# Splitting the rotary high-high terms of attention scores into pairs of half-array matmuls

## The chip, the core and the metric

The kernel runs on one core of a Trainium2 chip. The metric is the time of one execution on the device in microseconds (us). Engines are named as in the profile: PE is TensorE (matmuls), PEld its weight loads, DVE is VectorE, ACT is ScalarE, POOL is GpSimd, SP issues transfers.

## What is computed

One layer of an encoder: an RMS norm, one input projection, three token mixers (a convolution, a retention with two scan directions, latent attention), a gate, an output projection with the residual, a last RMS norm; 1024 tokens, 1024 channels, float32. The change touches the scores of the latent attention alone (8 heads, 1024 queries by 1024 keys):

```
def attend(blk):
    qn, qr = blk
    s = (jnp.einsum('bqhd,bkhd->bhqk', qn, k_nope)     # 128 channels per head
         + jnp.einsum('bqhr,bkr->bhqk', qr, k_rope))   # 64 rotary channels, key shared by all heads
    p = jax.nn.softmax(s.astype(jnp.float32) * scale, axis=-1).astype(v.dtype)
    return jnp.einsum('bhqk,bkhd->bqhd', p, v)
```

## The kernel before

Every float32 matmul operand is held as two fp32r tiles, high and low: the high tile is a cast, the low tile the rest (`split_l` on DVE). A product is then the sum of high-high, high-low and low-high passes into one PSUM bank (`mm3`, lines 174 to 176). A *pass* below is one matmul of a 128x128 stationary tile over 512 moving columns, together with its own weight load.

The program first computes the input projection with the convolution and the retention, then the attention, then the output projection. The attention is a loop over 16 units (`Unit`, line 795): unit u has head u // 2 and query half u % 2, which is four blocks of 128 queries. For each block t, `qk` makes the scores S, a PSUM tile of two banks, one bank for each half of 512 keys (j = 0, 1). A bank takes five passes: three for the 128 plain channels (L811 to L813: high-high, high-low, low-high) and two for the 64 rotary channels (L814, L815). The rotary operands use 128 array rows for 64 channels: the tile `Q2` (named QA or QB in the trace, by head) holds the low part of the query in rows 0 to 63 and its high part in rows 64 to 127. `K2` holds the key's high part in rows 0 to 63 and its low part in rows 64 to 127, and `K3` the other way round. So the pass with K2 gives low-high plus high-low, the pass with K3 low-low plus high-high. In the trace K2 and K3 are both called K.

After the second bank DVE takes the row maximum (L818), ACT the exponential with the row sums (L820), PE transposes the probabilities (`tr`, L829, two lots of four 128x128 transposes), ACT and DVE split them into PH and PL. The product with the values (`pvs`, mm3) and the normalization (`norm`, with one transpose of a 128x4 tile, L841) of a unit run in the next unit. `g_kr` (line 718) makes K2 and K3 once; `g_r` and `g_r2` make the rotated query tiles of a head pair; `slot_plan` spreads these and the projections of the next heads over the units.

The order that a reader of the code sees is not the order that runs: a scheduler puts the instructions of each engine into a row of its own. S has two buffers (of two banks), the transposes have two. The program gives every matmul a tile of the array: 128x128 for all but the 20 transposes of narrow tiles (16 of L841), which have 128x32.

Of the kernel before, what the change touches and what calls it, by code (L numbers as in the profile page):

```python
# [8 lines left out]
F32 = mybir.dt.float32  # L9
# [10 lines left out]
HS = 512  # L20
# [35 lines left out]
def body(tc, xT, x, w_in, w_uqn, w_uqr, w_uk, w_uv, w_out, vecs, decay, final_g,  # L56
         t_ret, t_mla, t_idx, t_iota, idm, out):
    nc = tc.nc
    act, dve, pool, pe, sp = nc.scalar, nc.vector, nc.gpsimd, nc.tensor, nc.sync

    def stt(eng, o, a, s, b, op0, op1):
        eng.scalar_tensor_tensor(o, a, s, b, op0=op0, op1=op1)  # L62
# [4 lines left out]
    def split_l(eng, lo, src, hi, scale=1.0):  # L67
        stt(eng, lo, src, scale, hi.bitcast(F32), MUL, SUB)
# [8 lines left out]
    def ps(tag, w=HS):  # L77
        cnt[0] += 1
        return psp[0].tile([P, w], F32, name=f"ps{cnt[0]}", tag=tag, bufs=PSB[tag])
# [13 lines left out]
    def mk(pl, shape, dt=F32, tag=None, bufs=None):  # L93
        cnt[0] += 1
        kw = {} if bufs is None else {"bufs": bufs}
        return pl.tile(shape, dt, name=f"{tag}{cnt[0]}", tag=tag, **kw)
# [569 lines left out]
    def half(i):  # L666
        return slice(i * HS, (i + 1) * HS)
# [42 lines left out]
    K2 = mk(at, [P, S], F32R, tag="K2")  # L710
    K3 = mk(at, [P, S], F32R, tag="K3")
    kk, qq, q2, vv = {}, {}, {}, {}
# [5 lines left out]
    def g_kr():  # L718
        for h in range(2):
            o = ps_up()  # L720
            pe.matmul(o, i2, krt[h], start=True, stop=True)
            act.copy(K2[0:64, half(h)], o[0:64])
            act.copy(K3[64:128, half(h)], o[64:128])
            split_l(dve, K2[64:128, half(h)], o[64:128], K3[64:128, half(h)])
            split_l(dve, K3[0:64, half(h)], o[0:64], K2[0:64, half(h)])

    def ps_up():
        tag = PRO_.pop(0) if PRO_ else "up"
        return ps(tag, 2 * HS)[:, :HS] if tag == "S" else ps(tag)
# [65 lines left out]
    class Unit:  # L795
# [6 lines left out]
        def qk(self, i):  # L802
            t, j = i // 2, i % 2
            if j == 0:
                self.S = ps("S", 2 * HS)
            kh, kl = kk[self.h, j]
            qh, ql = qq[self.h, self.qh]
            Q2 = q2[self.h, self.qh]
            ts = slice(t * P, (t + 1) * P)
            o = self.S[:, half(j)]  # L810
            pe.matmul(o, qh[:, ts], kh, start=True, stop=False)  # L811
            pe.matmul(o, qh[:, ts], kl, start=False, stop=False)  # L812
            pe.matmul(o, ql[:, ts], kh, start=False, stop=False)  # L813
            pe.matmul(o, Q2[:, ts], K2[:, half(j)], start=False, stop=False)  # L814
            pe.matmul(o, Q2[:, ts], K3[:, half(j)], start=False, stop=True)  # L815
            if j == 1:
                nm = mk(at, [P, 1], tag="nm", bufs=4)
                dve.tensor_reduce(nm, self.S, axis=AX.X, op=MAX, negate=True)  # L818
                p = mk(at, [P, S], tag="P", bufs=P_BUFS)
                act.activation(p, self.S, AF.Exp, bias=nm, accum_out=self.rs[:, t:t + 1])  # L820
                self.p.append(p)

        def tr(self, t, j):
            if t == 0:
                self.PT[j] = [mk(at, [P, 4, HS], F32R, tag=g, bufs=PT_BUFS) for g in ("PH", "PL")]
            ph, pl = (v[:, :, t * P:(t + 1) * P] for v in self.PT[j])
            o = ps("pp")
            for c in range(4):
                pe.transpose(o[:, c * P:(c + 1) * P], self.p[t][:, (4 * j + c) * P:(4 * j + c + 1) * P], ident)  # L829
            o = o.rearrange("p (c q) -> p c q", c=4)  # L830
            act.copy(ph, o)  # L831
            split_l(dve, pl, o, ph)
# [37 lines left out]
    for i in range(QT):  # L870
        lat(i, 1)
    g_q(0, 0)
    g_kr()
    g_r2(0, 0)
    g_r(0, 1)
# [4 lines left out]
    def slot_plan(u):  # L880
        p, r = u // 4, u % 4
        a, b = 2 * p, 2 * p + 1
        last = p == MH // 2 - 1
        if r == 0:
            return {0: [lambda: W.update({("k", b): lw_k(b)}), lambda: g_q(a, 1)],
                    4: [lambda: g_v(p, 1)], 5: [lambda: g_v(p, 2)],
                    6: [lambda: W.update({("q", b): lw_q(b)})],
                    7: [lambda: g_v(p, 3)]}
        if r == 1:
            d = {0: [lambda: g_k(b, 0)], 1: [lambda: g_k(b, 1)], 4: [lambda: g_q(b, 0)]}  # L890
            if not last:
                d[2] = [lambda: W.update({("r", p + 1): lw_r(p + 1)})]
                d[6] = [lambda: g_r(p + 1, 0)]
                d[7] = [lambda: W.update({("v", p + 1): lw_v(p + 1)})]
            return d
        if r == 2:
            d = {0: [lambda: g_q(b, 1)]}
            if not last:
                d[1] = [lambda: g_r2(p + 1, 0), lambda: W.update({("k", a + 2): lw_k(a + 2)})]
                d[4] = [lambda: g_k(a + 2, 0)]  # L900
                d[5] = [lambda: W.update({("q", a + 2): lw_q(a + 2)})]
                d[6] = [lambda: g_k(a + 2, 1)]
            return d
        if last:
            return {}
        return {0: [lambda: g_r(p + 1, 1)], 1: [lambda: g_v(p + 1, 0)], 4: [lambda: g_q(a + 2, 0)],
                5: [lambda: g_r2(p + 1, 1)]}

    fg_y = {}
    NUN = 2 * MH  # L910
    prev = None
    for u in range(NUN):
        cur = Unit(u)
        plan = slot_plan(u)
        if u == NUN - 1:
            sxx.close()
            wtx.close()
            latx.close()
            pax = ExitStack()
            pa = pax.enter_context(tc.tile_pool(name="pa", bufs=1, reuse_waits="tile", side="right"))  # L920
            woH = [mk(pa, [P, D], F32R, tag=f"woH{k}") for k in range(NWA)]
            woL = [mk(pa, [P, D], F32R, tag=f"woL{k}") for k in range(NWA)]

            rp = [pa, 1, 1]

            def wo_load(k):
                t = mk(rp[0], [P, D], tag="wor", bufs=rp[1])
                sp.dma_start(t, w_out[k * P:(k + 1) * P, :])
                act.copy(woH[k], t)
                split_l(dve, woL[k], t, woH[k])  # L930

            def y_load(hf, k):
                if rp[0] is not pa and k % 2:
                    t = mk(fin, [P, HS], tag="g", bufs=2)
                else:
                    t = mk(rp[0], [P, HS], tag="yr", bufs=rp[2])
                pool_ = pa if k % 8 < NYA else rp[0]
                hi = mk(pool_, [P, HS], F32R, tag=f"yh{k % 8}")
                lo = mk(pool_, [P, HS], F32R, tag=f"yl{k % 8}")
                sp.dma_start(t, y_dram[k][:, half(hf)])  # L940
                act.copy(hi, t)
                split_l(dve, lo, t, hi)
                fg_y[hf, k] = hi, lo

            plan = {1 + k: [lambda k=k: wo_load(k), lambda k=k: y_load(0, k)] for k in range(NWA)}
        for i in range(8):
            cur.qk(i)
            t, j = (i // 2 - 1) % 4, i % 2
            if i < 2:
                if prev:  # L950
                    prev.tr(t, j)
                    if j == 1:
                        prev.norm()
            else:
                if prev and i in (2, 3):
                    prev.pvs(j)
                cur.tr(t, j)
                if prev and i == 3:
                    prev.fin()
            for f in plan.get(i, []):  # L960
                f()
        prev = cur
    SB = [("S",), ("S",), ("pp", "pp"), ("pv", "up")]

# [187 lines left out]
```

## Time and profile before

| what | value |
|---|---|
| time, median of 3 runs | 1124.5 us (1123.42 to 1127.64) |
| profiled execution, its own time | 1124.83 us |
| its span in the trace | 1123.0 us |
| PE busy | 98% |
| DVE, ACT, POOL busy | 65%, 37%, 14% |

The profiled execution lasts 1.8 us longer than its span, and is 0.3 us above the median. Its PE rows give for every matmul a start and a modelled end. Since a matmul ends by this model after the next one has started, the cost of one in a stream is read from start to start, not from its duration.

### The profile page before, as it was taken

What the parts mean: (1) busy time and instruction counts of PE and PEld (TensorE: products, weight loads), DVE (VectorE), ACT (ScalarE), POOL (GpSimd) and SP (SyncE); (2) the same over time, 40 slices, a digit from 0 to 9 for tenths busy, and PEclk for the clock granted to TensorE, in tenths of its full rate; (3) what the DMA queues carried; (4) which work ended last, traced back from release to release, by engine and by line L of the source; (5) the groups of instructions that cost most, each with busy time, mean ns of one, the idle gap of its engine ahead of it and who ended that gap; (6) DMA issues with size and microseconds to landing.
All of it is one profiled execution on the core that took longest, in us unless ns stands there. A gap on an engine that the chain in (4) does not pass through costs nothing.

```text
span 1123.0 us, 14301 instructions
## 1 busy us (share of the span) xinstructions
PE 1100.7 (98%) x5568; PEld 923.3 (82%) x5568; DVE 726.4 (65%) x1004; ACT 412.9 (37%) x741; POOL 159.2 (14%) x141
## 2 busy tenths in 40 slices
PE   9999999999999999998899999999999999999997
PEld 7888888887898899886687888888888877888886
DVE  7599999998747785755665655655555573535033
ACT  8211221121144134223554644554554462424022
POOL 0200000213302442024201200210210000001000
PEclk9999999998999999999899999999999999999999
DMA  7321233220263122226302111211111140835113
GB/s 270 94 61 62 85 107 109 85 101 31 84 215 106 48 76 72 89 76 216 103 22 68 55 34 50 61 34 45 50 48 39 57 141 31 307 104 170 56 40 110
DMA packets 45620, 101.33 MB, mean 90 GB/s; under 512 B 5616, under 2 KB 9568, under 8 KB 45552
## 3 DMA queue, kind: packets, MB, share of 16 engines
q1 hardware_dynamic: 45504, 100.35, 27.1%
q8 instruction: 43, 0.70, 0.3%
q14 instruction: 25, 0.20, 0.1%
q0 software_dynamic: 48, 0.08, 0.1%
HBM read 74.14 MB, written 24.17 MB: 88 GB/s over the span
## 4 chain that ended last, share of the span: by engine, by line
PE 94%; DVE 2%; DMA 1%; ACT 1%; issue 1%; SPq 0%; POOL 0%; POOLq 0%; DVEq 0%; ACTq 0%
PE ps L174 24%; PE ps L175 24%; PE ps L176 24%; PE ps L829 4%; PE ps L811 3%; PE ps L815 3%; PE ps L814 3%; PE ps L813 3%; PE ps L812 3%; PE ps L299 1%; PE ps L575 1%; PE ps L564 1%; PE ps L579 1%; PE ps L577 1%; DMA hp<-in_xT_dram 1%
## 5 line engine op out<-in xcount | busy, mean ns | idle before, releaser
L175 PE MATMUL ps<-xL,wh 128*128 128x512 f32 (+1 forms) x612 | 239.1, 391 | 0.1
L176 PE MATMUL ps<-xH,wl 128*128 128x512 f32 (+1 forms) x612 | 238.8, 391 | 0.0
L174 PE MATMUL ps<-xH,wh 128*128 128x512 f32 (+1 forms) x612 | 237.1, 394 | 1.5 <-ACT xH L138 1.0
L62 DVE SCALAR_TENSOR_TENSOR acc<-hp,cwh,acc 128x1024 f32<-128x1024 f32 x120 | 154.0, 1323 | 0.1
L174 PEld LDWEIGHTS ps<-xH,wh 128*128 128x128 f32 x612 | 115.6, 190 | 25.4 <-ACT xH L138 1.2
L175 PEld LDWEIGHTS ps<-xL,wh 128*128 128x128 f32 x612 | 115.9, 189 | 24.0 <-DVE xL L62 0.6
L176 PEld LDWEIGHTS ps<-xH,wl 128*128 128x128 f32 x612 | 115.5, 189 | 23.9 <-issue 0.2
L62 DVE SCALAR_TENSOR_TENSOR PL<-ps,PH 128x512 fp32r<-128x512 f32 x128 | 85.7, 685 | 54.4 <-ACT PH L831 54.0
L831 ACT CAST PH<-ps 128x512 fp32r<-128x512 f32 x128 | 73.0, 589 | 93.7 <-PE ps L829 93.1
L175 PE MATMUL ps<-woL,yh 128*128 128x512 f32 (+1 forms) x264 | 100.9, 386 | 0.0
L818 DVE TENSOR_REDUCE nm<-ps 128x1 f32<-128x1024 f32 x64 | 78.1, 1221 | 34.2 <-PE ps L815 33.6
L176 PE MATMUL ps<-woH,yl 128*128 128x512 f32 (+1 forms) x264 | 100.2, 386 | 0.0
L174 PE MATMUL ps<-woH,yh 128*128 128x512 f32 (+1 forms) x264 | 100.0, 386 | 0.0
L165 ACT CAST wh<-wraw 128x1024 fp32r<-128x1024 f32 x40 | 42.0, 1053 | 123.7 <-PE ps L175 114.2
L820 ACT ACTIVATE P<-ps,nm 128x1024 f32<-128x1024 f32 x64 | 71.7, 1120 | 29.3 <-DVE nm L818 27.0
L829 PE MATMUL ps<-ident,P 128*128 128x128 f32 x512 | 72.7, 272 | 0.0
L829 PEld LDWEIGHTS ps<-ident,P 128*128 128x128 f32 x512 | 61.5, 140 | 12.5 <-DVE PL L62 0.6
L175 PEld LDWEIGHTS ps<-woL,yh 128*128 128x128 f32 x264 | 49.6, 188 | 10.4
L62 DVE SCALAR_TENSOR_TENSOR wl<-wraw,wh 128x1024 fp32r<-128x1024 f32 (+2 forms) x45 | 54.3, 1206 | 5.9 <-ACT wh L165 5.1
L174 PEld LDWEIGHTS ps<-woH,yh 128*128 128x128 f32 x264 | 49.6, 188 | 10.4
L176 PEld LDWEIGHTS ps<-woH,yl 128*128 128x128 f32 x264 | 49.6, 188 | 10.3
L65 POOL TENSOR_TENSOR g<-g,rb 128x512 f32<-128x512 f32 x16 | 21.2, 1322 | 255.0 <-DMA rb<-rs_dram 255.0
(292 smaller groups left out, 2035.3 us busy)
## 6 DMA issues: line engine op xcount, KB each, us to landing
wraw<-in_w_in_dram SPq DMA_DIRECT2D x40, 512.0 KB, 3.5
wor<-in_w_out_dram SPq DMA_DIRECT2D x16, 512.0 KB, 5.2
g_dram<-ga SPq DMA_DIRECT2D x29, 256.0 KB, 2.2
yr<-y_dram SPq DMA_DIRECT2D x18, 256.0 KB, 3.7
g<-g_dram SPq DMA_DIRECT2D x16, 256.0 KB, 3.1
rb<-rs_dram SPq DMA_DIRECT2D x16, 256.0 KB, 3.1
y_dram<-osb SPq DMA_DIRECT2D x16, 256.0 KB
z<-in_x_dram SPq DMA_DIRECT2D x8, 512.0 KB, 3.4
```

What stands on the lines that cost most here:

```text
L62: eng.scalar_tensor_tensor(o, a, s, b, op0=op0, op1=op1)
L165: act.copy(hi, t)
L174: pe.matmul(o, sh, mh, start=first, stop=False, skip_group_check=skip)
L175: pe.matmul(o, sh, ml, start=False, stop=False, skip_group_check=skip)
L176: pe.matmul(o, sl, mh, start=False, stop=last, skip_group_check=skip)
L811: pe.matmul(o, qh[:, ts], kh, start=True, stop=False)
L812: pe.matmul(o, qh[:, ts], kl, start=False, stop=False)
L813: pe.matmul(o, ql[:, ts], kh, start=False, stop=False)
L818: dve.tensor_reduce(nm, self.S, axis=AX.X, op=MAX, negate=True)
L820: act.activation(p, self.S, AF.Exp, bias=nm, accum_out=self.rs[:, t:t + 1])
L829: pe.transpose(o[:, c * P:(c + 1) * P], self.p[t][:, (4 * j + c) * P:(4 * j + c + 1) * P], ident)
L831: act.copy(ph, o)
```

## The change

In `g_kr` the two splits that wrote the key's low part into K3[0:64] are gone. K3[0:64] now holds a second copy of the query's high part, moved to rows 0 to 63, 512 columns for each query half; the new method `hi0` writes it with one ACT copy per unit, for unit 0 ahead of the loop and for unit u + 1 in slot 4 of unit u. In `qk` a bank takes four full passes (plain channels, and K2 for the two cross terms); the pass with K3 is gone, and with it the low-low term. Once both banks have theirs, two matmuls of 64 array rows each add the high-high terms: rows 64 to 127 (Q2 and K3, L816) for the first bank, rows 0 to 63 (the copy of the query and K2, L817) for the second.

```diff
             act.copy(K2[0:64, half(h)], o[0:64])
             act.copy(K3[64:128, half(h)], o[64:128])
             split_l(dve, K2[64:128, half(h)], o[64:128], K3[64:128, half(h)])
-            split_l(dve, K3[0:64, half(h)], o[0:64], K2[0:64, half(h)])
...
-            pe.matmul(o, Q2[:, ts], K2[:, half(j)], start=False, stop=False)
-            pe.matmul(o, Q2[:, ts], K3[:, half(j)], start=False, stop=True)
+            pe.matmul(o, Q2[:, ts], K2[:, half(j)], start=False, stop=False, skip_group_check=True)
             if j == 1:
+                q0 = K3[0:64, self.qh * HS:(self.qh + 1) * HS]
+                pe.matmul(self.S[:, :HS], Q2[64:128, ts], K3[64:128, :HS], start=False, stop=True, skip_group_check=True)
+                pe.matmul(o, q0[:, ts], K2[0:64, HS:], start=False, stop=True, skip_group_check=True)
...
+        def hi0(self):
+            act.copy(K3[0:64, self.qh * HS:(self.qh + 1) * HS], q2[self.h, self.qh][64:128].bitcast(F32))
...
+    nxt_u = Unit(0)
+    nxt_u.hi0()
     for u in range(NUN):
-        cur = Unit(u)
+        cur = nxt_u
...
             for f in plan.get(i, []):
                 f()
+            if i == 4 and u < NUN - 1:
+                nxt_u = Unit(u + 1)
+                nxt_u.hi0()
```

The program gives the two new matmuls the array tiles 64x128 at row 64 and 64x128 at row 0. It has 64 of each. In PE's row 59 times an L817 stands right behind an L816; the other five L816 and five L817 have full-array work on both sides, or (once) the L817 of another block ahead.

PE, the scores of the third block of unit 0. K_4337 is K2 and K_4338 is K3; kH_4346 and kL_4347 belong to the first key half, kH_4392 and kL_4393 to the second. Before:

```order
L811 MATMUL ps_4563<-kH_4346,qH_4438 128x512
L812 MATMUL ps_4563<-kL_4347,qH_4438 128x512
L813 MATMUL ps_4563<-kH_4346,qL_4439 128x512
L814 MATMUL ps_4563<-K_4337,QA_4459 128x512
L815 MATMUL ps_4563<-K_4338,QA_4459 128x512
L811 MATMUL ps_4563<-kH_4392,qH_4438 128x512
L812 MATMUL ps_4563<-kL_4393,qH_4438 128x512
L813 MATMUL ps_4563<-kH_4392,qL_4439 128x512
```

After:

```order
L810 MATMUL ps_4562<-kH_4346,qH_4438 128x512
L811 MATMUL ps_4562<-kL_4347,qH_4438 128x512
L812 MATMUL ps_4562<-kH_4346,qL_4439 128x512
L813 MATMUL ps_4562<-K_4337,QA_4457 128x512
L810 MATMUL ps_4562<-kH_4392,qH_4438 128x512
L811 MATMUL ps_4562<-kL_4393,qH_4438 128x512
L812 MATMUL ps_4562<-kH_4392,qL_4439 128x512
L813 MATMUL ps_4562<-K_4337,QA_4457 128x512
L816 MATMUL ps_4562<-K_4338,QA_4457 128x512
L817 MATMUL ps_4562<-K_4337,K_4338 128x512
```

Before, L814 and L815 of the second bank follow, ten full passes in all; now there are eight, and the pair L816, L817 behind them.

PE, the end of the scores of the first two blocks of unit 0 (ps_4495 and ps_4530 before, ps_4494 and ps_4529 after). Before:

```order
L814 MATMUL ps_4495<-K_4337,QA_4459 128x512
L815 MATMUL ps_4495<-K_4338,QA_4459 128x512
L814 MATMUL ps_4530<-K_4337,QA_4459 128x512
L815 MATMUL ps_4530<-K_4338,QA_4459 128x512
L811 MATMUL ps_4530<-kH_4392,qH_4438 128x512
L812 MATMUL ps_4530<-kL_4393,qH_4438 128x512
L813 MATMUL ps_4530<-kH_4392,qL_4439 128x512
```

After:

```order
L813 MATMUL ps_4494<-K_4337,QA_4457 128x512
L816 MATMUL ps_4494<-K_4338,QA_4457 128x512
L813 MATMUL ps_4529<-K_4337,QA_4457 128x512
L810 MATMUL ps_4529<-kH_4392,qH_4438 128x512
L811 MATMUL ps_4529<-kL_4393,qH_4438 128x512
L812 MATMUL ps_4529<-kH_4392,qL_4439 128x512
L813 MATMUL ps_4529<-K_4337,QA_4457 128x512
L816 MATMUL ps_4529<-K_4338,QA_4457 128x512
L817 MATMUL ps_4494<-K_4337,K_4338 128x512
L817 MATMUL ps_4529<-K_4337,K_4338 128x512
```

The last matmul of the first block moved behind the scores of the second.

ACT, where the first query tile is made (xh, QA and QB are steps of `g_r2`, xr the next step of `g_r`, P the first exponential). Before:

```order
L769 CAST xh_4457<-xr_4406 128x512
L773 CAST QA_4459<-xh_4457 64x512
L774 CAST QB_4460<-xh_4457 64x512
L757 COPY xr_4475<-ps_4465 128x512
L820 ACTIVATE P_4528,rs_4494<-ps_4495,nm_4526 128x1024
```

After:

```order
L768 CAST xh_4455<-xr_4406 128x512
L772 CAST QA_4457<-xh_4455 64x512
L773 CAST QB_4458<-xh_4455 64x512
L825 CAST K_4338<-QA_4457 64x512
L756 COPY xr_4473<-ps_4463 128x512
L821 ACTIVATE P_4527,rs_4492<-ps_4494,nm_4525 128x1024
```

The copy of `hi0` (L825) stands ahead of the evacuation of the next rotary projection.

## Rows read from the trace of the kernel before

**Rows 1.** The page: busy time, then the chain that ended last, by engine.

```profile
PE 1100.7 (98%) x5568; PEld 923.3 (82%) x5568; DVE 726.4 (65%) x1004; ACT 412.9 (37%) x741; POOL 159.2 (14%) x141
...
PE 94%; DVE 2%; DMA 1%; ACT 1%; issue 1%; SPq 0%; POOL 0%; POOLq 0%; DVEq 0%; ACTq 0%
```

**Rows 2.** Busy time by stretch (stretch, length, engines, PE clock, DMA): the attention.

```profile
560.00:960.00 400.00, 395.42 (x2062) 328.15 (x2061) 229.29 (x324) 202.52 (x384) 46.17 (x36) 1.00 0.18 53
```

**Rows 3.** Groups by line and form (busy us, mean ns, idle before): half of K3's passes.

```profile
L815 PE MATMUL ps<-K,QA 128*128 128x512 f32 x64 | 25.7, 402 | 0.0
```

**Rows 4.** Timeline (start us, us, engine, line): passes, weight loads, and one narrow transpose.

```profile
658.76 0.39 PE L813 MATMUL ps<-kH,qL 128*128 128x512 f32 x1
658.76 0.19 PEld L814 LDWEIGHTS ps<-K,QA 128*128 128x128 f32 x1
658.99 0.39 PE L814 MATMUL ps<-K,QA 128*128 128x512 f32 x1
658.99 0.19 PEld L815 LDWEIGHTS ps<-K,QA 128*128 128x128 f32 x1
659.21 0.39 PE L815 MATMUL ps<-K,QA 128*128 128x512 f32 x1
...
659.44 0.40 PE L174 MATMUL ps<-PH,vH 128*128 128x512 f32 x1
659.44 0.08 PEld L841 LDWEIGHTS ps<-ident,rs 128*4 128x4 f32 x1
...
659.67 0.27 PE L841 MATMUL ps<-ident,rs 128*4 128x128 f32 x1
659.68 0.19 PEld L175 LDWEIGHTS ps<-PL,vH 128*128 128x128 f32 x1
659.70 0.48 PE L175 MATMUL ps<-PL,vH 128*128 128x512 f32 x1
...
660.02 0.40 PE L176 MATMUL ps<-PH,vL 128*128 128x512 f32 x1
```

**Rows 5.** Timeline of PE: eight full-size transposes between passes.

```profile
643.81 0.39 PE L176 MATMUL ps<-lH,wlq 128*128 128x512 f32 x1
644.04 1.03 PE L829 MATMUL ps<-ident,P 128*128 128x128 f32 x8
644.89 0.50 PE L811 MATMUL ps<-kH,qH 128*128 128x512 f32 x1
645.23 0.39 PE L812 MATMUL ps<-kL,qH 128*128 128x512 f32 x1
```

**Rows 6.** Timeline of PEld: the two weight loads behind those transposes.

```profile
644.89 0.19 PEld L811 LDWEIGHTS ps<-kH,qH 128*128 128x128 f32 x1
645.00 0.19 PEld L812 LDWEIGHTS ps<-kL,qH 128*128 128x128 f32 x1
```

**Rows 7.** Waits of PE (who <- for whom: us in total, times, longest): two of 13.

```profile
PE ps L814 <- DVE QA L62: 1.9, 1, 1.9
...
PE ps L174 <- DVE K L62: 0.3, 1, 0.3
```

**Rows 8.** Instructions that write QA (min/median/max ns): the ACT copy.

```profile
L773 ACT CAST QA<-xh x8: 617/618/622, 551.7 to 833.5; 64x512 fp32r<-64x512 f32 x8
```

**Rows 9.** Timeline of PE where the scores begin.

```profile
554.00 0.63 PE L813 MATMUL ps<-kH,qL 128*128 128x512 f32 x1
554.43 0.63 PE L814 MATMUL ps<-K,QA 128*128 128x512 f32 x1
...
556.47 0.39 PE L812 MATMUL ps<-kL,qH 128*128 128x512 f32 x1
```

**Rows 10.** Busy time by stretch, as in rows 2: the same place.

```profile
552.40:556.20 3.80, 3.69 (x10) 2.89 (x11) 1.37 (x2) 1.13 (x2) 0.00 (x0) 0.57 0.39 108
```

**Rows 11.** The page's costliest groups, as in rows 3: row maximum and exponential.

```profile
L818 DVE TENSOR_REDUCE nm<-ps 128x1 f32<-128x1024 f32 x64 | 78.1, 1221 | 34.2 <-PE ps L815 33.6
...
L820 ACT ACTIVATE P<-ps,nm 128x1024 f32<-128x1024 f32 x64 | 71.7, 1120 | 29.3 <-DVE nm L818 27.0
```

More of the change, by code (lines that the diff above doesn't have):

```diff
@@ L810, in qk @@
             o = self.S[:, half(j)]
-            pe.matmul(o, qh[:, ts], kh, start=True, stop=False)
-            pe.matmul(o, qh[:, ts], kl, start=False, stop=False)
-            pe.matmul(o, ql[:, ts], kh, start=False, stop=False)
-            pe.matmul(o, Q2[:, ts], K2[:, half(j)], start=False, stop=False)
-            pe.matmul(o, Q2[:, ts], K3[:, half(j)], start=False, stop=True)
+            pe.matmul(o, qh[:, ts], kh, start=True, stop=False, skip_group_check=True)
+            pe.matmul(o, qh[:, ts], kl, start=False, stop=False, skip_group_check=True)
+            pe.matmul(o, ql[:, ts], kh, start=False, stop=False, skip_group_check=True)
+            pe.matmul(o, Q2[:, ts], K2[:, half(j)], start=False, stop=False, skip_group_check=True)
             if j == 1:
+                q0 = K3[0:64, self.qh * HS:(self.qh + 1) * HS]
+                pe.matmul(self.S[:, :HS], Q2[64:128, ts], K3[64:128, :HS], start=False, stop=True, skip_group_check=True)
+                pe.matmul(o, q0[:, ts], K2[0:64, HS:], start=False, stop=True, skip_group_check=True)
                 nm = mk(at, [P, 1], tag="nm", bufs=4)
```

## The prediction

> **What bounds the kernel now.** I read the page first: PE is busy 98% of the span, and the chain that ended last runs through PE for 94% of it, while DVE, ACT and POOL have 65%, 37% and 14% [rows 1]. Then the stretch that the change touches: from 560 to 960 us, nearly all of the attention, PE is busy 395.4 of 400.0 us at the full clock, DVE 229.3 and ACT 202.5 [rows 2]. So 4.6 us of PE idleness are all that other engines cost here, and the stage takes what PE's stream takes. What an instruction costs in that stream is read from start to start. In the scores a pass begins 0.23 us after the one before (658.76, 658.99, 659.21), and the weight load of the next pass begins when the current one does [rows 4]. The mean duration of K3's passes, 402 ns [rows 3], is a modelled end, some 0.16 us after the next pass has begun, and must not be multiplied by a count.
>
> A weight load alone can follow another after 0.11 us (644.89, 645.00) [rows 6]. Of the 0.23 us of a pass it fills less than half, which is why it is hidden.
>
> **Removed.** 128 full passes on K3, 64 with QA [rows 3] and as many with QB, each 0.23 us in the stream: 29.4 us of PE time. With them go two of four DVE splits in `g_kr`. PE waits 0.3 us once for a split into K, ahead of a rotary projection [rows 7]; I take that 0.3 us as gained.
>
> **Added on PE.** 128 matmuls of 64 array rows over 512 columns. Ten of them have no partner beside them and take a pass each, 0.23 us. The other 118 are 59 pairs, and the price of a pair decides everything. No row shows two matmuls streaming at the same time, nor one on 64 rows, so I bound it.
> - Below: each half still streams 512 columns, and no 512-column pass in rows 4 is quicker than 0.23 us. A pair cannot cost less than that.
> - Above, without a cost of switching: one after the other, 0.46 us.
> - Between: if the second half's weight load begins only when the first half's matmul begins, as every weight load in rows 4 does, the second half can begin 0.11 us late [rows 6], and the pair costs 0.34 us.
> - Beyond: a cost for going from 128 array rows to 64 and back. What a full stop could cost I take from the modelled end: 0.39 us duration against 0.23 us spacing leaves 0.16 us until the last result is out [rows 4], once going in and once coming out.
>
> The nearest row on switching is L841, whose tile in the program is 128x32, with 128x128 work on both sides. It begins 0.23 us after the pass ahead of it, the ordinary spacing, so going in costs nothing. From its start to the second pass behind it (659.67 to 660.02) are 0.35 us; less the 0.23 us of the pass between, 0.12 us [rows 4]. Eight full-size transposes between passes take 645.23 - 643.81 = 1.42 us less two passes of 0.23: 0.96, or 0.12 us each [rows 5]. The narrow one costs what an ordinary one does; the switch is not to be seen in either direction. So I take no cost of switching, and keep 2 x 0.16 us for the range.
>
> The Trainium skill (TensorEngine Tiling (Array Packing), Key Properties) says the opposite: "Changing tiling mode (not just tile) drains the TensorE". On column tiles the trace does not bear it out, as the narrow transpose shows; on row tiles no run here shows it. If it held, the third rival below is what it would do.
>
> For the overlap I take the low end, 0.23 us. The two halves share neither array rows nor SBUF partitions nor a bank, and the one thing that rows 4 show them sharing, the weight load's path, has 0.12 us of each pass free: room for a second load of 0.11 us under the last K2 pass. That this room can be used is the assumption; the first rival is that it cannot.
>
> **Added elsewhere.** ACT gets 16 copies of 64x512, 0.62 us each by the like copy into QA [rows 8], 9.9 us in all. ACT has 197 us free in the attention [rows 2], so they lie beside PE's work; each runs half a unit or more ahead of its use. If ACT were the late engine, they would cost up to 9.9 us. The exception is the first one: it stands ahead of the xr copy and the first exponential, and PE's L817 of the first block waits for it. That L817 is 12 matmuls behind the first K2 pass, at least 2.8 us later at 0.23 us each, and the copy ends some 1.3 us after QA is made (QB's copy and its own, 0.62 us each), so this wait is covered.
>
> **Moved.** Of the first two blocks the first is complete only behind the scores of the second. There the clock is granted at 0.57 [rows 10], between 1.2 and 2.4 GHz, after PE had waited 1.9 us for QA [rows 7], and passes are 0.43 us apart until about 556 us [rows 9]. The first row maximum starts some six matmuls later, that is 1.4 us at full clock to 2.6 us at half clock. Nine passes (2.1 us) stand between the scores and the first transposes, while maximum and exponential need 1.2 and 1.1 us [rows 11] plus their hand-overs. I put 0.5 us on the wait that this can open, an estimate from these rows. At four other places one to seven rows stand inside a pair; with S in two buffers I take nothing for them.
>
> **The sum**, against the profiled execution's own 1124.8 us: minus 29.4 (128 passes x 0.23), plus 2.3 (10 lone halves), plus 13.6 (59 pairs x 0.23), minus 0.3, plus 0.5, which is -13.3 or about 1111.5 us. The profiled execution lies 0.3 us above the median of 1124.5, less than any of these roundings, so I forecast **1111.5 us** for the median, 1.2% faster.
>
> **Rivals.**
> 1. *The second weight load is late.* A pair costs 0.34 us; 59 x 0.11 = 6.5 us of the gain go: 1118 us. For it: every weight load in rows 4 begins with the matmul ahead of it, never before. Against: with full-array tiles the one spare set of weights is taken until then, so these rows cannot tell a rule from a lack of room; halves of the array may each have their own.
> 2. *The change does not do what it says:* the halves run one after the other and nothing is gained, 59 x 0.23 = 13.6 us more than the sum: 1125 us. For it: in no row do two matmuls share time. A part overlap whose gain goes into switching (0.1 to 0.2 us per run of half-array work) lands here too.
> 3. *PE stops at each switch of the tile*, the mechanism that ends on the other side. There are 59 pairs and nine separate places for the ten lone halves, 68 runs of half-array work. At 2 x 0.16 us each that is 21.8 us on top of the sum: 1133 us. If the weight load behind each stop lies bare too, 0.11 us twice, 15 us more: 1148 us. It makes the kernel slower than before once going in and coming out cost over 13.3 / 68 = 0.20 us together. For it: nothing in the trace, and the row tile is a form that the trace lacks. Against: L841.
>
> A fourth, that a faster PE runs into DVE or ACT, is small: after the change they would be busy some 59% and 55% of the attention by rows 2.
>
> **How the numbers follow.** Chances: the forecast 0.38, the late weight load 0.22, no gain 0.20, the stops 0.20. About 0.5% (5.6 us) is what a measurement of this kernel can tell from no change, so faster means below 1118.9 us and slower above 1130.1. Faster is all of the forecast but 0.01 and 0.16 of the first rival, 0.53. Slower is the stops and 0.02 of the no-gain case, 0.22. The rest, 0.25, is within 0.5%. The likeliest case by itself would give 1109 to 1114. Most of the chance lies between it and 1125; the stops begin at about 1131 and go far, so a range of 1109 to 1133 us takes in the first three cases and the lower part of the fourth, and leaves out some 0.17.
>
> **What the profile of the changed kernel would show.** From the start of the last K2 pass ahead of a pair to the start of the work behind it: two spacings, 0.46 us, if the forecast is right; 0.57 if the second load is late; 0.69 if the halves do not overlap; 0.78 and more with stops. The second half's weight load begins before the first half's matmul in the first case only. L841's spacing stays. PE's idle time from 560 to the end of the attention stays near 4.6 us; more than 3 us on top would mean that ACT's copies or the later row maxima matter, and my zero there was wrong. Everything ahead of 540 us should take as long as before. What would make the prediction wrong as a whole is a price of a pair that lies outside 0.23 to 0.46 us.

## The result and the profile after

The changed kernel takes 1140.84 us (median of 4 runs, 1139.2 to 1142.08) against 1123.96 us before (four runs now; the first three had 1124.5 in the median): a ratio of 1.0147, 95% interval 1.0126 to 1.0169. It is slower by 1.5%, where 1.2% faster was forecast. The profiled execution has a span of 1137.4 us, 14.4 us longer than before; its own time is 1139.2 us.

The page of the changed kernel, busy time and the chain by engine, as in [rows 1]:

```profile
PE 1114.2 (98%) x5568; PEld 908.4 (80%) x5568; DVE 725.8 (64%) x1002; ACT 423.0 (37%) x757; POOL 158.6 (14%) x141
...
PE 91%; DMA 3%; DVE 2%; ACT 2%; issue 1%; SPq 1%; POOL 0%; POOLq 0%; DVEq 0%; ACTq 0%
```

The same number of matmuls keeps PE busy 13.5 us longer. Nothing else took over: DVE is as busy as before, ACT has the 10 us of copies on top. The stretch of [rows 2] in the changed kernel:

```profile
560.00:960.00 400.00, 395.28 (x2002) 302.91 (x2001) 228.06 (x321) 211.22 (x397) 46.63 (x36) 1.00 0.17 51
```

PE is busy in as much of it as before (395.42 then) and at the full clock, but in 400 us it gets through 2002 matmuls in place of 2062. In this stretch PE does not wait more; its stream is slower. Where it is slower is seen in the timeline of one block of scores (start us, us, engine, line), to be held against [rows 4]:

```profile
660.46 0.40 PE L812 MATMUL ps<-kH,qL 128*128 128x512 f32 x1
660.47 0.19 PEld L813 LDWEIGHTS ps<-K,QA 128*128 128x128 f32 x1
660.70 0.39 PE L813 MATMUL ps<-K,QA 128*128 128x512 f32 x1
661.02 0.18 PEld L816 LDWEIGHTS ps<-K,QA 64*128 64x128 f32 x1 [0.36 <-issue]
661.02 0.50 PE L816 MATMUL ps<-K,QA 64*128 64x512 f32 x1
661.02 0.18 PEld L817 LDWEIGHTS ps<-K,K 64*128 64x128 f32 x1
661.02 0.50 PE L817 MATMUL ps<-K,K 64*128 64x512 f32 x1
661.45 0.19 PEld L174 LDWEIGHTS ps<-PH,vH 128*128 128x128 f32 x1 [0.24 <-issue]
661.45 0.49 PE L174 MATMUL ps<-PH,vH 128*128 128x512 f32 x1
...
661.58 0.08 PEld L845 LDWEIGHTS ps<-ident,rs 128*4 128x4 f32 x1
661.78 0.27 PE L845 MATMUL ps<-ident,rs 128*4 128x128 f32 x1
```

Two things stand here. The two halves start together, weight loads and matmuls, all at 661.02: the overlap that the forecast assumed is there. And around them PE stops. The pair begins 0.32 us after the pass ahead of it (660.70), not 0.23. Its weight load, which in a full-array stream would have begun at 660.70, begins with the pair, so that nothing hides it (below, such a load is called bare). The weight load behind the pair begins 0.43 us after the pair (661.45), again together with its matmul and not one pass earlier. The matmul after that follows at 0.33 us, not 0.23. From 660.70 to 661.78 are 1.08 us for three spacings (into the pair, from the pair to the work behind it, and on to the next), 0.69 us if nothing stopped.

Over the whole trace: 18 pairs have full passes on both sides, and the distance from the pass ahead to the second matmul behind is 1.096 us in the median; three lone halves have 1.089. Less 0.69 that is **0.40 us for each run of half-array work** (a run is an unbroken row of half-array matmuls), whether one half is in it or two. There are 68 runs: 27 us. The pair saves one pass, 0.23 us, and so it loses 0.17 us each time. In front of transposes the stop is a little cheaper: for 25 pairs the third transpose behind begins 1.019 us after the pass ahead, against 0.908 us in the kernel full_array below, where two full passes stand in the same place. There a pair loses 0.11 us and the stop costs 0.34, so the 68 runs are nearer 26 us than 27.

To place the loss I measure a stage, from the last matmul of L721 (the rotary keys) to the last transpose of the probabilities. Before, from the lines' own views (min/median/max ns, first and last start):

```profile
L721 PE MATMUL ps<-kr,i x4: 592/592/593, 537.3 to 543.6; 128*128 128x512 f32 x4
...
L829 PE MATMUL ps<-ident,P x512: 270/272/328, 559.5 to 950.1; 128*128 128x128 f32 x171
```

After (the transposes are now L833):

```profile
L721 PE MATMUL ps<-kr,i x4: 590/592/592, 538.3 to 544.6; 128*128 128x512 f32 x4
...
L833 PE MATMUL ps<-ident,P x512: 270/272/330, 561.3 to 965.4; 128*128 128x128 f32 x171
```

The stage grew from 406.5 to 420.8 us, by 14.3 of the span's 14.4. The busy times of the engines in it (PE's first), before and after:

```profile
543.60:950.10 406.50, 398.30 (x2066) 329.55 (x2064) 235.65 (x333) 207.82 (x393) 50.85 (x39) 1.00 0.18 53
...
544.60:965.40 420.80, 411.52 (x2067) 313.94 (x2065) 235.44 (x331) 217.62 (x409) 51.17 (x39) 0.99 0.17 51
```

So 13.2 us of the growth are PE's busy time and 1.1 us are waits (9.3 us without work against 8.2). Not all of the 13.2 us are stops. Near the end of the attention PE waits 1.1 us for PL and 0.9 us for an exponential, and right behind these waits the granted clock falls from 2.4 GHz to 1.2 for a part of this stretch:

```profile
930.00:935.00 5.00, 4.64 (x13) 3.03 (x14) 3.07 (x6) 2.88 (x7) 0.00 (x0) 0.66 0.50 151
```

In the kernel before, the clock is 1.00 there. A clock of 0.66 over 5 us costs at most 1.7 us, an estimate.

What lies ahead of the stage varies by some us from one execution to the next (its beginning lies between 540 and 547 us in all the traces here, though nothing in front of it was changed), so below the stage of the profiled execution stands beside each time. A stage comes from one execution of each kernel, so small differences between stages prove little by themselves.

### The profile page after: what moved, and what is told of

Same layout as the page of the kernel before. It is cut to its first block, busy times and chain, and to the rows that moved or that the text cites. A ratio compares the mean times of both kernels' runs of the same rounds, so it can differ in the third digit from the quotient of the medians.

```text
span 1137.4 us, 14319 instructions
## 1 busy us (share of the span) xinstructions
PE 1114.2 (98%) x5568; PEld 908.4 (80%) x5568; DVE 725.8 (64%) x1002; ACT 423.0 (37%) x757; POOL 158.6 (14%) x141
## 4 chain that ended last, share of the span: by engine, by line
PE 91%; DMA 3%; DVE 2%; ACT 2%; issue 1%; SPq 1%; POOL 0%; POOLq 0%; DVEq 0%; ACTq 0%
PE ps L174 24%; PE ps L175 23%; PE ps L176 23%; PE ps L833 5%; PE ps L810 3%; PE ps L812 3%; PE ps L813 3%; PE ps L811 2%; PE ps L816 2%; DMA wor<-in_w_out_dram 1%; PE ps L299 1%; ACT P L821 1%; PE ps L575 1%; DMA wr<-in_w_uqr_dram 1%; PE ps L564 1%
## 5 line engine op out<-in xcount | busy, mean ns | idle before, releaser
L833 PE MATMUL ps<-ident,P 128*128 128x128 f32 x512 | 75.3, 276 | 1.2 <-DVE PL L62 1.1
L833 PEld LDWEIGHTS ps<-ident,P 128*128 128x128 f32 x512 | 59.6, 140 | 17.6 <-issue 6.8
```

## The experiments

Theory: PE stops when its array goes from 128 rows to 64 and back; the halves themselves overlap. Rival A: a half-array matmul is dear by itself, or the halves do not overlap. Rival B: the loss is in the order, the later row maxima and ACT's copies.

| kernel | median us | ratio to before, 95% | stage us |
|---|---|---|---|
| before | 1124 | | 406.5 |
| changed | 1140.84 | 1.0147 (1.0126 to 1.0169) | 420.8 |
| p_full | 1129.08 | 1.0043 (1.0020 to 1.0067) | 412.4 |
| p_col | 1131.95 | 1.0065 (1.0029 to 1.0100) | 412.7 |
| p_row | 1148.49 | 1.0213 (1.0153 to 1.0273) | 429.9 |
| one_half | 1133.81 | 1.0093 (1.0050 to 1.0136) | 417.9 |
| same_half | 1156.14 | 1.0278 (1.0256 to 1.0300) | 438.0 |
| full_array | 1126.64 | 1.0027 (1.0010 to 1.0045) | 409.5 |
| full_no_copies | 1125.34 | 1.0022 (1.0009 to 1.0036) | 409.4 |
| grouped | 1128.85 | 1.0042 (1.0028 to 1.0055) | 413.0 |
| grouped_later | 1130.65 | 1.0072 (1.0047 to 1.0097) | 414.7 |

### The price of a switch by itself

Three kernels add to the kernel before one small matmul of 16 columns behind each block, and differ in its array tile and the parts of the operands that go with it: 128x128 (p_full), 128x32 (p_col), 64x128 (p_row). Each kernel has one of the last three lines; the labels behind them are not in the code.

```diff
+    Z0 = mk(at, [P, 16], tag="Z0")
+    dve.memset(Z0, 0.0)
+    Z = mk(at, [P, 16], F32R, tag="Z")
+    act.copy(Z, Z0)
...
+            if j == 1:
+                pe.matmul(o[:, :16], Q2[:, ts], Z, start=False, stop=True, skip_group_check=True)                 # p_full
+                pe.matmul(o[0:32, :16], Q2[:, t * P:t * P + 32], Z, start=False, stop=True, skip_group_check=True)  # p_col
+                pe.matmul(o[:, :16], Q2[64:128, ts], Z[64:128], start=False, stop=True, skip_group_check=True)     # p_row
```

p_full. 

> The kernel before with one more matmul behind the scores of each of the 64 blocks: 128 array rows, 128 columns of weights, 16 moving columns of zeros, added into the first 16 columns of the second bank. It is the control for the two kernels beside it. Every theory expects the price of a bare weight load, about 0.11 us each as for the narrow transposes: 64 x 0.11 = 7 us, so about 1131 us.

p_row. 

> The same small matmul on 64 array rows (rows 64 to 127) in place of 128. Theory (PE stops when it goes from 128 array rows to 64 and back, by the trace of the change about 0.40 us for both ways on top of the streaming): 64 x about 0.43 = 27 us, so about 1151 us. Rival A (a half-array matmul is slow in its streaming, or the halves do not overlap, and the switch costs nothing): 16 columns stream in no time, so 1131 us as the control. Rival B (the loss is in the order, the later row maxima or the copies of the change, none of which are here): 1131 us.

p_col. 

> The same small matmul with all 128 rows and 32 columns of weights, array tile 128x32 as the narrow transposes have. If every change of the array tile makes PE stop: 1151 us as with 64 rows. If only a change of the rows does, as the narrow transposes of the kernel before suggest: the control's 1131 us or a little less.

The timeline of PE around one of them, p_full:

```profile
652.44 0.39 PE L819 MATMUL ps<-K,QA 128*128 128x512 f32 x1
652.67 0.17 PE L821 MATMUL ps<-Z,QA 128*128 128x16 f32 x1
652.70 0.48 PE L817 MATMUL ps<-kH,qL 128*128 128x512 f32 x1
653.01 0.39 PE L818 MATMUL ps<-K,QA 128*128 128x512 f32 x1
```

p_col:

```profile
651.66 0.40 PE L819 MATMUL ps<-K,QA 128*128 128x512 f32 x1
651.89 0.17 PE L821 MATMUL ps<-Z,QA 128*32 128x16 f32 x1
651.92 0.48 PE L817 MATMUL ps<-kH,qL 128*128 128x512 f32 x1
652.24 0.39 PE L818 MATMUL ps<-K,QA 128*128 128x512 f32 x1
```

p_row:

```profile
653.38 0.40 PE L819 MATMUL ps<-K,QA 128*128 128x512 f32 x1
653.70 0.27 PE L821 MATMUL ps<-Z,QA 64*128 64x16 f32 x1
653.91 0.50 PE L817 MATMUL ps<-kH,qL 128*128 128x512 f32 x1
654.24 0.39 PE L818 MATMUL ps<-K,QA 128*128 128x512 f32 x1
```

From the pass ahead to the second one behind: 0.57, 0.58 and 0.86 us; in the median of 26 such places each 0.572, 0.572 and 0.866. Less the two passes (0.46), the small matmul costs 0.11 us with the full array, 0.11 us on 32 columns of weights and 0.41 us on 64 rows. The stages follow: 5.9 and 6.2 us longer than before for the first two, 23.4 for p_row (64 x 0.41 = 26). Against its control p_full, p_row's stage is 17.5 us longer, and 64 x 0.29 are 18.6. The medians (p_full, p_row, p_col) came out at 1129.1, 1148.5 and 1132.0 us where 1131, 1151 and 1131 were expected. So the switch costs 0.29 us more than the bare weight load that any short matmul leaves, it is paid without any pair, any copy or any new order, and a change from 128 columns to 32 does not pay it. Rival B cannot explain p_row, and rival A's long streaming is not in it.

### Do the halves overlap?

one_half drops the second matmul (L817).

```diff
-                q0 = K3[0:64, self.qh * HS:(self.qh + 1) * HS]
-                pe.matmul(o, q0[:, ts], K2[0:64, HS:], start=False, stop=True, skip_group_check=True)
```

> The changed kernel without the second half-array matmul (L817): the high-high term of the second key half is left out. Theory (the halves overlap fully, and a run of half-array work costs one pass plus the stops, however many halves are in it): as slow as the changed kernel but for the four runs fewer (64 in place of 68), 4 x 0.6 = 2 us, so about 1138 us. Rival A (no overlap): 64 x 0.23 = 15 us quicker than the changed kernel, about 1126 us. Rival B: unchanged, about 1140 us.

Its lone half stands in PE's stream like this:

```profile
658.98 0.39 PE L813 MATMUL ps<-K,QA 128*128 128x512 f32 x1
...
659.30 0.50 PE L815 MATMUL ps<-K,QA 64*128 64x512 f32 x1
659.72 0.50 PE L174 MATMUL ps<-PH,vH 128*128 128x512 f32 x1
660.06 0.27 PE L843 MATMUL ps<-ident,rs 128*4 128x128 f32 x1
```

658.98 to 660.06 is 1.08 us, as around the pair (1.08 above); the median of 22 is 1.084 against the pairs' 1.096. The second half costs 0.01 us. The stage is 2.9 us shorter than the changed kernel's, near the 2.5 us (4 x 0.63) of the four runs that are missing. The median, 1133.8 us, came out lower than the 1138 that was expected; in the profiled executions 4.2 of the 7.1 us between the two lie ahead of the stage (it begins at 540.4 and 544.6 us), where the kernels do the same. Rival A's 1126 us lies outside the interval (1129.5 to 1139.2 us).

same_half puts both terms on the same 64 rows, so that they can't share the array.

```diff
-                q0 = K3[0:64, self.qh * HS:(self.qh + 1) * HS]
...
-                pe.matmul(o, q0[:, ts], K2[0:64, HS:], start=False, stop=True, skip_group_check=True)
+                pe.matmul(o, Q2[64:128, ts], K3[64:128, HS:], start=False, stop=True, skip_group_check=True)
```

> The changed kernel with both high-high terms on the same 64 rows (64 to 127), without the 16 copies: as many stops, but the two cannot share the array. Theory (the pair overlaps fully): 59 pairs become 59 x 0.21 to 0.23 us longer, 12 to 14 us, so about 1153 us. Rival A (the pair did not overlap in the first place): the changed kernel's 1140 us.

The expectation says "without the 16 copies", but the edit leaves them in: `hi0` still runs, and ACT has 409 instructions in the stage as in the changed kernel. Nobody reads what they write.

```profile
660.01 0.40 PE L813 MATMUL ps<-K,QA 128*128 128x512 f32 x1
660.34 0.50 PE L815 MATMUL ps<-K,QA 64*128 64x512 f32 x1
660.68 0.39 PE L816 MATMUL ps<-K,QA 64*128 64x512 f32 x1
661.00 0.50 PE L812 MATMUL ps<-kH,qL 128*128 128x512 f32 x1
661.34 0.40 PE L813 MATMUL ps<-K,QA 128*128 128x512 f32 x1
```

Now the second half begins 0.34 us after the first, of which 0.11 are the first half's bare weight load and 0.23 a pass. From the pass ahead to the second one behind are 1.33 us in place of 1.08; the median of 19 such runs is 1.320 against 1.096, so the second half costs 0.22 us where it can't overlap. The time rose by 15.3 us over the changed kernel's (12 to 14 expected), the stage by 17.2. 59 x 0.22 us are 13; part of the rest is the clock, which is granted at 0.50 from 555 to 565 us here, against 0.66 from 555 to 560 and 1.00 behind in the changed kernel. Rival A falls: the pair of the change did overlap.

### The order and the copies alone

full_array keeps the place of the two matmuls and the copies, but gives them 128 rows again, and with them the low-low term.

```diff
+    KX = mk(at, [64, S], F32R, tag="KX")
...
+            split_l(dve, K3[0:64, half(h)], o[0:64], K2[0:64, half(h)])
...
-                q0 = K3[0:64, self.qh * HS:(self.qh + 1) * HS]
-                pe.matmul(self.S[:, :HS], Q2[64:128, ts], K3[64:128, :HS], start=False, stop=True, skip_group_check=True)
-                pe.matmul(o, q0[:, ts], K2[0:64, HS:], start=False, stop=True, skip_group_check=True)
+                pe.matmul(self.S[:, :HS], Q2[:, ts], K3[:, :HS], start=False, stop=True, skip_group_check=True)
+                pe.matmul(o, Q2[:, ts], K3[:, HS:], start=False, stop=True, skip_group_check=True)
...
-            act.copy(K3[0:64, self.qh * HS:(self.qh + 1) * HS], q2[self.h, self.qh][64:128].bitcast(F32))
+            act.copy(KX[:, self.qh * HS:(self.qh + 1) * HS], q2[self.h, self.qh][64:128].bitcast(F32))
```

> The changed kernel with its two half-array matmuls put back on 128 rows (Q2 with K3, whose low half is made again), still behind the scores of both banks; the 16 copies of the change go to a tile of their own, which nobody reads. What stays of the change is its order and its copies. Theory (the stops at a change of the array's rows are the whole loss): the time of the kernel before, 1124 us, within 2 us. Rival B (order, later row maxima, copies on ACT): near the changed kernel, 1135 to 1141 us.

full_no_copies is the same without the 16 copies.

```diff
-    nxt_u.hi0()
...
-                nxt_u.hi0()
```

> The kernel with the high-high terms back on 128 rows behind both banks, now also without the 16 copies on ACT. What is left of the change is the place of the last two passes of a block. If the copies caused the 2 to 3 us that the version with copies is above the kernel before: 1124 us, as before. If the place of the passes did (row maxima later, PE waiting for the exponential and for the transposes' buffers): 1126 to 1127 us, as with the copies.

With the rows undone the loss is nearly gone: 1.0027 with the copies, 1.0022 without. The copies cost nothing that can be told. What is left of it belongs to the place of the last two passes: 1 to 5 us by the intervals, 3.0 and 2.9 us by the stages, a little more than the 2 us that the theory had allowed. PE's waits show some of it (who, for whom, us, times, longest). Before:

```profile
PE ps L811 <- ACT P L820: 0.7, 1, 0.7
```

In full_no_copies:

```profile
PE ps L811 <- ACT P L821: 1.8, 3, 1.0
...
PE ps L833 <- DVE PL L62: 1.5, 1, 1.5
```

The wait for the exponential is 1.1 us longer than in the kernel before, and PE's wait in the transposes for PL was not there. The longest of each lies near the end of the attention, and behind them the clock falls as in the changed kernel: it is granted at 0.78 from 915 to 920 us in full_no_copies and at 0.79 from 920 to 925 in full_array, where the kernel before has 1.00. In the stage of full_no_copies PE is without work 1.1 us longer than before and busy 1.8 us longer, in that of full_array 2.3 and 0.7. In the changed kernel the like waits are:

```profile
PE ps L813 <- DVE QA L62: 3.7, 1, 3.7
PE ps L810 <- ACT P L821: 1.6, 3, 0.9
...
PE ps L833 <- DVE PL L62: 1.1, 1, 1.1
```

### Fewer stops

grouped keeps the whole computation and puts two pairs into one run: an odd block begins with its pair (b0, b1, which start its two banks), next to the pair that ends the block before it (a0, a1). The dependencies fix their order on PE.

```diff
...
             if j == 1:
...
+                if not odd:
+                    self.nS = ps("S", 2 * HS)
+                    b0, b1 = self.pair(self.nS, t + 1, True)
+                    a0, a1 = self.pair(self.S, t, False)
+                    for x, y in ((b0, last), (b1, b0), (a0, b1), (a1, a0)):
+                        tc.add_manual_dep(x.ins, y.ins.name, mybir.DependencyInfo(
+                            mybir.DependencyClass.NoSync, mybir.DependencyReason.DATA), reason="order")
```

> The changed kernel with the pairs of two blocks put together: an odd block begins with its pair (which starts its two banks), right ahead of the pair that ends the block before it. All arithmetic is kept. 34 runs of half-array work in place of 68, 30 of them with four matmuls. Theory (a stop of 0.40 us per run, none between matmuls of the same tile size): 34 x 0.40 = 13.6 us less than the changed kernel, about 1126 us, as long as before or a little less. Rival A (each half-array matmul is dear by itself) and rival B (later row maxima): the changed kernel's 1138 to 1141 us.

```profile
600.22 0.40 PE L822 MATMUL ps<-K,QB 128*128 128x512 f32 x1
600.54 0.18 PEld L805 LDWEIGHTS ps<-K,QB 64*128 64x128 f32 x1 [0.36 <-issue]
600.54 0.49 PE L805 MATMUL ps<-K,QB 64*128 64x512 f32 x1
...
600.55 0.49 PE L806 MATMUL ps<-K,K 64*128 64x512 f32 x1
600.65 0.19 PEld L805 LDWEIGHTS ps<-K,QB 64*128 64x128 f32 x1
...
600.88 0.39 PE L805 MATMUL ps<-K,QB 64*128 64x512 f32 x1
600.88 0.39 PE L806 MATMUL ps<-K,K 64*128 64x512 f32 x1
601.21 0.50 PE L819 MATMUL ps<-kH,qH 128*128 128x512 f32 x1
601.54 0.39 PE L820 MATMUL ps<-kL,qH 128*128 128x512 f32 x1
```

From 600.22 to 601.54 are 1.32 us: four pass times (0.92) and one stop of 0.40, with two pairs in it; 15 such runs have 1.320 in the median. The second pair's weight load begins at 600.65, under the first pair, so between the pairs nothing stops: the 0.34 us from 600.54 to 600.88 are the first pair's bare load (0.11) and one pass (0.23). The time fell by 12.0 us, of 13.6 expected, back to 0.42% above the kernel before. That is the strongest sign for the theory, since the halves, the copies and the number of matmuls stayed. By PE's stream alone this kernel should tie with the one before or be a little faster (63 passes saved are 14.5 us, 34 stops cost 13.6). Its stage is 6.5 us longer all the same. PE is without work for 13.0 us of it, against 8.2 before; the longest waits in the stage are:

```profile
PE ps L822 <- DVE QA L62: 4.2, 1, 4.2
...
PE ps L819 <- ACT P L834: 3.1, 1, 3.1
```

With each of the two the clock falls: it is granted at 0.50 from 550 to 555 us (0.79 before) and at 0.73 from 925 to 930 (1.00 before).

grouped_later leaves unit 0 as in the change, to see whether the first scores are where the rest goes.

```diff
+            self.grp = u > 0
...
+            odd = t % 2 and self.grp
...
+                if not self.grp:
+                    self.pair(self.S, t, False)
+                elif not odd:
```

> The grouped kernel, but with unit 0 as in the change (each block ends with its own pair), so that the first scores are not held back by the start of the next block. 35 runs of half-array work. By the stops alone it should take 128 x 0.23 = 29.4 us off the kernel before and put 64 pairs x 0.23 and 35 x 0.40 back, about 29 us: 1124 us. If the waits at the first scores were what kept the grouped kernel 4 to 5 us above that: 1125 to 1126 us. If the waits are spread over the attention: 1128 to 1129 us as the grouped kernel.

It took 1130.65 us, no less than grouped and more than any of the three times expected. So the first block's arrangement is not where the rest goes. PE is without work for 12.4 us of its stage, it still waits 3.9 us for QA, and the clock is at 0.69 from 550 to 555 us, 0.63 from 555 to 560 and 0.77 from 925 to 930. So the remaining 5 to 8 us of the grouped kernels are waits at the two ends of the attention and the slower clock that goes with them; how they divide, and what in the order causes the waits, was not settled. No version was found that beats the kernel before. Even without those waits a run of two pairs gains 2 x 0.23 - 0.40 = 0.06 us, some 2 us in all 32, and S has buffers for two blocks only; longer runs were not tried.

## Why the prediction was wrong

- **What bounds the kernel:** right. PE's stream sets the time before and after, and the stage's growth is PE's.
- **Removed, 29.4 us:** right as far as the traces tell. Full passes are 0.23 us apart as before (a median of 0.232 from 560 to 920 us, 0.231 before), and PE's 0.3 us wait for K is gone from its waits.
- **The pair at 0.23 us:** right in its streaming, a point where no row of before could help. The second half costs 0.01 us (one_half) and 0.22 us where it can't overlap (same_half). The first rival, the late second weight load, falls: both loads begin at once. But the reason that was given for the overlap did not hold. The second load was to find room under the last K2 pass; in the trace neither load begins there (660.70), both begin with the pair (661.02). That the pair came out at one pass was luck as far as that reason goes.
- **No cost of switching: the step that failed.** The prediction took the narrow transpose L841 as the nearest row, a tile of 128x32, and carried its zero over to a tile of 64x128. L841's row was read rightly: p_col shows the same for a matmul, 0.11 us on 32 columns as on 128. But a change of columns and a change of rows do not cost the same, and p_row shows 0.41 us. The term should have been 68 x 0.40 = 27 us in place of 0. The sum as it stood, -13.3, becomes +13.9 with it; the stage grew by 14.3. That the two lie so close is in part luck: with 0.34 us in front of transposes the term is nearer 26, and 1.1 us of waits and up to 1.7 us of the slower clock at the end of the attention make up for it. With the stop the price of a pair is 0.23 + 0.40 = 0.63 us, outside the 0.23 to 0.46 that the prediction had set for itself.
- **The third rival** (PE stops at each switch of the tile) is what happened. Its price was 2 x 0.16 us, 0.54 with bare weight loads; 0.40 was measured, and its parts can be read from the timeline: 0.09 us late going in, then a bare weight load (0.11), and the same again coming out. What in PE makes it late is not shown. From the last K2 pass to the work behind the pair are 0.75 us (660.70 to 661.45), nearer to this rival's 0.78 than to any other's. It named 0.20 us as the point where the change turns slower. I gave it 0.20, and the range stopped at 1133 us, the low end of the 1133 to 1148 us that this rival itself had given.
- The Trainium skill (TensorEngine Tiling (Array Packing), Key Properties) says that a change of tiling mode drains TensorE. For rows the trace agrees, at 0.40 us a run; for 128x32 tiles it shows no cost (0.11 us, as with the full array). The prediction let the second half of that finding speak against the rule as a whole.
- **Moved, 0.5 us:** a wait did open, but neither its place nor its size was as forecast. The place of the passes costs about 3 us by the stages of full_array and full_no_copies, and the waits for the exponential and for PL that show it lie at the end of the attention, not at the first blocks. At the first scores PE's wait for QA is 3.7 us in place of 1.9 [rows 7], but in the whole stage of the changed kernel it is without work only 1.1 us longer than before.
- **ACT's copies at nothing:** right, 1.0027 with and 1.0022 without them.

The runs leave one thing open. The medians are 16.9 us apart and the profiled executions 14.4; the 2.5 us between were not traced. The profiled execution is the fastest of the four of the changed kernel.

## What to carry to other kernels

Before packing two 64-row matmuls beside one another, count the runs of half-array work, not the matmuls: each run costs two stops, here 0.40 us, against 0.23 us gained per pair, so a run has to hold at least two pairs to break even. Take the price of an array mode from a row of the same kind (rows from rows, columns from columns), or keep the whole range of the rival that says otherwise. A small matmul of 16 columns, added once per block to the kernel that already runs, would have given the price in one run.

## What was not expected of the hardware

- With fp32r operands two 64-row matmuls on different halves of the array start at the same moment, and so do their weight loads (661.02 all four); the pair streams in the time of one (1.096 us against 1.084 from pass to pass).
- A weight load for a tile of 64 rows is not begun when the last pass of 128 rows begins: the profile has it 0.32 us later (660.70, 661.02), where the load of a full-array tile begins with the pass ahead (660.46, 660.47).
- A tile of 128x32 among 128x128 ones costs 0.11 us for 16 columns, as the full array does; one of 64x128 costs 0.41 us.
- Between matmuls of 64 rows there is no stop, on the same half (same_half) or on both: the second pair of a run begins 0.34 us after the first (600.54, 600.88), 0.11 of which are the first pair's bare weight load, and the whole run of four has one stop of 0.40 us.
